# Six output tiles accumulated during the first modulation, x normed in place, and a final turn by transposes

## The chip, the cores and the metric

The kernel runs on one core of one Trainium2 chip. The metric is device time in microseconds. PE is TensorE, DVE VectorE, ACT ScalarE, POOL GpSimd, and SP the engine whose queue issues all loads and stores.

## What is computed

One inference step of a backbone of two layers over 384 tokens: 128 context tokens and 256 latent ones, width 1024, all in fp32.

```
mod = silu(cond) @ w_mod + b_mod              # shift, scale, gate, twice; per layer
h   = rmsnorm(x) * (1 + scale1) + shift1
q, k, v, gates, conv inputs, merge gates = h @ w_in
mix = sum over 3 branches of sigmoid(merge gate) * branch(h)   # DeltaNet, short conv, attention
x   = x + gate1 * rmsnorm(mix @ w_out)
x   = x + gate2 * rmsnorm(relu(h2 @ w_up)**2 @ w_down)         # h2 like h, from x
```

Outputs are y for all tokens, and keys, values and DeltaNet states of the context tokens. Nothing of h can be made before the modulation of its channels, and every other product of a layer needs h.

## The kernel before

**Products.** Each large product is made of three fp32r products: a high and a low half of the weights (wh, wl) and of the activations (HH, HL, or ah, al) give high x high, high x low and low x high. The functions FM (channels on the partitions, 8 x 3 products of 384 columns for one output tile), TM (tokens on the partitions; keys and values have 272 columns) and TMW record them. `fetch` loads a chunk of weights into wr (4 buffers), ACT casts the high half and DVE subtracts the low one (3 buffers each). All products write to 8 PSUM banks: 4 called mm, 4 called ax.

**Opening of layer 0.** `setup` loads the condition, x (8 tiles xt of 128 channels by 384 tokens) and constants. `first_norm` squares the tiles on ACT, adds them up in turn on DVE and POOL, and takes means by PE; `bcast` spreads the inverse norm into a bank (rb). `modquarter(q)` makes shift and scale for two channel tiles: 16 matmuls of 256 columns, with the condition as stationary operand in one of four column groups of the array, whose weights come as six loads (ws) through 8 buffers; `finish` copies the sums to rows and turns them with small products against sel2. `make_h(k)` makes h of tile k. The first FM tiles (keys, queries and values of head 0) have their products recorded tile by tile behind the four quarters. `turn_x` transposes x into tokens (om) behind the second quarter. Constants that are needed later are loaded once the last modulation matmul has been made (`hold`).

**Order.** All work is recorded first; a list scheduler (`schedule`) then gives every engine a fixed order, by the priority of a class (crit, st, gemm, ev, w, bg and others), by modelled durations (`cost`) and by a modelled transfer: rate, latency and issue time of the queue. On the chip an engine executes in that order and waits for what is late. While nothing else can run ahead of the first large product, and at three other places, PE makes filler products on ones.

**Body.** Behind keys and values come the heads: DeltaNet on DVE and POOL in small steps, and between them PE work from a list (`fills`): query groups, gates of the attention branch (`evac_mg` keeps their tanh in xt), branch projections. Then `split` makes high (ACT) and low halves (POOL) of the DeltaNet output ot, `merge` combines, w_out and the MLP follow. Modulation pieces for later stages are summed in between, partly on DVE (macc).

**End.** `post` takes the last product of a token block (OT), `newton` the inverse norm on single columns (ns), and `finish_y` turns x + gate * rmsnorm(...) back to channels: 8 products of x with the identity, 8 of the update with a diagonal matrix dg, accumulated in two banks, copied to yst and stored.

## Time and profile before

| what | us |
|---|---|
| median of 3 runs | 1985.2 (1985.07 to 1986.72) |
| the profiled execution | 1986.29 |
| its span, first to last instruction | 1984.6 |
| PE busy | 1957.0 |
| DVE busy | 1405.9 |

The span is what the views cover; start and times in them count from its first instruction. A busy PE includes the filler, and a product's time in a row is longer than its distance to the next one, since products are pipelined. All instructions have one line (L1778, where the recorded calls are made), so they are told apart by their tiles: `mm<-HH,wl` is a product into an mm bank from activations HH and low weights.

### The profile page before, as it was taken

The numbers are of one execution on the slowest core, as the hardware profiler recorded it, in microseconds if no ns is written. First come the engines' busy times: TensorE is split into PE (matmuls) and PEld (weight loads), VectorE is DVE, ScalarE is ACT, GpSimd is POOL, SyncE is SP. The second block draws the span as 40 slices with busy tenths as digits, with TensorE's granted clock in tenths as the row PEclk, the third lists the DMA queues.
The fourth block names the chain that finished last, engine by engine and source line by source line (L and its number), as shares of the span: only waits on it lengthen the run. The fifth ranks groups of instructions, "written<-read, shape, count | busy, mean of one in ns | idle before, by whom it ended". The sixth has DMA issues, their size and how long they took to land.

```text
span 1984.6 us, 35881 instructions
## 1 busy us (share of the span) xinstructions
PE 1957.0 (99%) x12980; PEld 1806.7 (91%) x12980; DVE 1405.9 (71%) x4317; ACT 949.3 (48%) x2188; POOL 431.6 (22%) x666
## 2 busy tenths in 40 slices
PE   9999999999999999999999999999999999999999
PEld 6998999999998799779779989999999998898987
DVE  3798887988868589769557988779888545432433
ACT  4676644555542354334246665445555424443432
POOL 1222222123234313003012022222232322110210
PEclk9999999999999999999999999999999999999999
DMA  8522333333336837756654223333333334554352
GB/s 270 192 81 84 106 110 130 119 122 117 107 124 208 289 128 231 217 189 204 158 177 147 85 94 115 111 119 122 121 115 107 120 123 144 195 124 128 127 128 64
DMA packets 132385, 280.48 MB, mean 141 GB/s; under 512 B 12240, under 2 KB 80496, under 8 KB 132208
## 3 DMA queue, kind: packets, MB, share of 16 engines
q1 hardware_dynamic: 132208, 278.19, 43.0%
q8 instruction: 102, 1.67, 0.3%
q14 instruction: 75, 0.61, 0.1%
HBM read 270.73 MB, written 7.42 MB: 140 GB/s over the span
## 4 chain that ended last, share of the span: by engine, by line
PE 83%; DVE 7%; DMA 4%; ACT 3%; issue 2%; POOL 0%; SPq 0%; DVEq 0%; ACTq 0%
PE mm L1778 70%; PE ax L1778 14%; DMA wr<-in_wmod 3%; DVE wl L1778 2%; DVE macc L1778 2%; ACT E L1778 1%; DVE q L1778 1%; ACT wh L1778 0%; DVE MB L1778 0%; ACT ht L1778 0%; ACT junk L1778 0%; DVE Xc L1778 0%; DVE Pr L1778 0%; DVE XT L1778 0%; DMA ws<-in_wmod 0%
## 5 line engine op out<-in xcount | busy, mean ns | idle before, releaser
L1778 DVE TENSOR_TENSOR wl<-wr,wh 128x1024 fp32r<-128x1024 f32 (+2 forms) x380 | 478.7, 1261 | 307.0 <-ACT wh L1778 305.8
L1778 ACT CAST wh<-wr 128x1024 fp32r<-128x1024 f32 (+2 forms) x380 | 396.0, 1043 | 559.3 <-PE mm L1778 454.1
L1778 PE MATMUL mm<-HH,wl 128*128 128x384 f32 x1664 | 568.9, 342 | 1.7 <-DVE wl L1778 1.7
L1778 PE MATMUL mm<-HL,wh 128*128 128x384 f32 x1664 | 567.7, 341 | 0.0
L1778 PE MATMUL mm<-HH,wh 128*128 128x384 f32 x1664 | 564.9, 340 | 0.6 <-ACT HH L1778 0.6
L1778 PEld LDWEIGHTS mm<-HH,wl 128*128 128x128 f32 x1664 | 312.9, 188 | 9.6 <-issue 4.5
L1778 PEld LDWEIGHTS mm<-HL,wh 128*128 128x128 f32 x1664 | 312.8, 188 | 6.5 <-issue 3.9
L1778 PEld LDWEIGHTS mm<-HH,wh 128*128 128x128 f32 x1664 | 312.4, 188 | 5.7 <-issue 1.2
L1778 DVE SCALAR_TENSOR_TENSOR macc<-wr,csil,macc 128x1024 f32<-128x1024 f32 x98 | 144.9, 1512 | 26.7 <-DMA wr<-in_wmod 26.7
L1778 PE MATMUL mm<-wh,HH 128*128 128x256 f32 (+1 forms) x480 | 139.9, 292 | 2.1 <-DVE eq L1778 1.4
L1778 PE MATMUL mm<-wl,HH 128*128 128x256 f32 (+1 forms) x480 | 139.4, 291 | 1.3 <-DVE wl L1778 1.3
L1778 PE MATMUL mm<-wh,HL 128*128 128x256 f32 (+1 forms) x480 | 140.1, 292 | 0.0
L1778 DVE TENSOR_TENSOR Pr<-MB,Xc 128x6 f32<-128x6 f32 (+30 forms) x496 | 138.7, 280 | 0.3
L1778 DVE TENSOR_REDUCE Xc<-Pr 128x6 f32<-128x12 f32 (+30 forms) x496 | 127.4, 257 | 7.7
L1778 DVE STREAM_SHUFFLE MB<-Mc 128x6 f32<-128x6 f32 (+30 forms) x496 | 131.7, 272 | 0.0
L1778 PE MATMUL mm<-al,wh 128*128 128x384 f32 x384 | 129.9, 339 | 1.6 <-POOL al L1778 1.5
L1778 PE MATMUL mm<-ah,wl 128*128 128x384 f32 x384 | 130.0, 339 | 0.2 <-DVE wl L1778 0.2
L1778 PE MATMUL mm<-ah,wh 128*128 128x384 f32 x384 | 130.0, 339 | 0.0
L1778 PE MATMUL mm<-wh,u 128*128 128x512 f32 x384 | 124.0, 399 | 0.0
L1778 PE MATMUL mm<-wh,ah 128*128 128x512 f32 x288 | 112.9, 392 | 0.0
L1778 PE MATMUL mm<-wh,al 128*128 128x512 f32 x288 | 112.7, 391 | 0.0
L1778 PE MATMUL mm<-wl,ah 128*128 128x512 f32 x288 | 112.5, 390 | 0.0
(270 smaller groups left out, 3314.8 us busy)
## 6 DMA issues: line engine op xcount, KB each, us to landing
wr<-in_wf SPq DMA_DIRECT2D x336, 512.0 KB, 3.3
wr<-in_wmod SPq DMA_DIRECT2D x80, 512.0 KB, 4.2
wr<-in_wq SPq DMA_DIRECT2D x16, 512.0 KB, 3.4
wr<-in_wdg SPq DMA_DIRECT2D x16, 512.0 KB, 3.3
ws<-in_wmod SPq DMA_DIRECT2D x16, 384.0 KB, 7.0
E<-scr SPq DMA_DIRECT2D x16, 384.0 KB, 3.6
Qe<-scr SPq DMA_DIRECT2D x16, 256.0 KB, 3.8
wr<-in_wkv SPq DMA_DIRECT2D x8, 408.0 KB, 5.7
```

Source lines behind the costliest of these rows:

```text
L1778: o.call(*o.a, **o.k)
```

## The change

Six output tiles (keys, queries, values of head 0, and three gates of the attention branch) are accumulated in six banks over the four quarters: `firstproducts(q)` makes the products of the two channel tiles of quarter q for all six, from two chunks of 768 columns (kind a), and evacuates them after the last quarter. The gates go out of the list of fills in layer 0. A modulation quarter loads all of one piece, then all of the other, into one bank. x is turned and then normed in place before the quarters, and h of context tokens is made on DVE, of latent tokens on ACT. Square sums are added in pairs and summed by PE. x comes in four loads, three constants come later.

Low halves of the DeltaNet output are made on DVE (`split_out`). In the second layer the three parts of the key weights are one group (`whole`). `finish_y` adds the residual on DVE and transposes the sum. The planner's model of transfers and of the small products is changed, and a class sp added. The diff, cut:

```diff
-                return n * 4 / 2.4 + 3 if op.k["tile_position"] == (0, 0) else 27.0
+                return n * 0.965 + 3 if op.k["tile_position"] == (0, 0) else 27.0
...
-    return max(56.0, n * outs[0].shape[0] * 4 / 360.0)
+    return max(56.0, n * outs[0].shape[0] * 4 / 385.0)
...
-    hw = 650.0
+    hw = 1000.0
...
-            dma = max(dma, hw + 650) + o.cost
+            dma = max(dma, hw + 1300) + o.cost
...
+        **{(e, "sp"): 1000 for e in ("ACT", "DVE")},
...
+        elif kind == "a":
+
+            src = aps["wf"][0, W_DK:W_DV + 1:8] if key[2] == 0 else aps["wf"][0, W_MG + 16:W_MG + 19]
+            src, n = src[:, :, 256 * key[1]:256 * key[1] + 256].rearrange("o p c -> p o c"), 768
...
-        dma = SP.dma_start(raw.rearrange("p (f c) -> p f c", f=4) if kind in "od" else raw[:, :n], src)
+        dma = SP.dma_start(raw[:, :n].rearrange("p (f c) -> p f c", c=256) if kind in "oda" else raw[:, :n], src)
...
-    def tok_means(ps, col, *srcs):
-
-        n = 3 * len(srcs)
-        for j, src in enumerate(srcs):
-            for t in range(3):
-                PE.matmul(ps[:, col:col + 3], lhsT=src[:, t * P:(t + 1) * P], rhs=sel[:, t, :],
-                          start=3 * j + t == 0, stop=3 * j + t == n - 1)
...
-    def split(k, src):
+    def split(k, src, eng=POOL):
         ACT.copy(a_hi[k], src)
-        POOL.tensor_tensor(out=a_lo[k], in0=src, in1=a_hi[k].bitcast(F32), op=SUB)
+        eng.tensor_tensor(out=a_lo[k], in0=src, in1=a_hi[k].bitcast(F32), op=SUB)
...
             def run(ch):
-                hi, lo = ch[0]
-                if j == 0:
+                if js[0] == 0:
...
                 for t in range(3):
                     ps = st["ps"][t]
                     rec.cls = "gemm"
-                    for i, k in enumerate(parts[j]):
...
+                    for (hi, lo), j in zip(ch, js):
+                        for i, k in enumerate(parts[j]):
+                            ah = h_hi[k][:, t * P:(t + 1) * P]
+                            al = h_lo[k][:, t * P:(t + 1) * P]
+                            wh, wl = hi[:, i * n:(i + 1) * n], lo[:, i * n:(i + 1) * n]
...
-        for j in range(len(parts)):
-            G([(kind, l, g, j)], part(j))
+        n_ = len(parts)
+        for js in [tuple(range(n_))] if whole else [(j,) for j in range(n_)]:
+            G([(kind, l, g, j) for j in js], part(js))
...
-        for k in range(8):
-            SP.dma_start(xt[k], aps["x"][:, k, :])
-        for t_, n_ in ((sel, "sel"), (ident, "ident"), (sel2, "sel2"), (bmod, "bmod"), (gn, "gn")):
+        for k in range(0, 8, 2):
+            SP.dma_start(XT[:, k:k + 2, :], aps["x"][:, k:k + 2, :])
+        for t_, n_ in ((sel, "sel"), (ident, "ident")):
...
+    def early_consts():
+        rec.cls = "w"
+        for t_, n_ in ((sel2, "sel2"), (bmod, "bmod"), (gn, "gn")):
+            SP.dma_start(t_, aps[n_])
+        rec.cls = "bg"
...
-        def run_part(j):
+        def run_part(p, j):
             def run(ch):
                 rec.cls = "st"
-                if j == 0:
-                    st["ps"] = axtile(), axtile()
+                if p + j == 0:
+                    st["ps"] = axtile()
                 for i, k in enumerate(KPARTS[j]):
                     c = k % 4
-                    for p in range(2):
-                        S["mm"] = PE.matmul(st["ps"][p][32 * c:32 * c + 32, :256], lhsT=csil[:, k, :],
-                                            rhs=ch[p][:, i], start=k < 4, stop=k > 3, tile_position=(0, 32 * c))
-                if j == 2:
+                    S["mm"] = PE.matmul(st["ps"][32 * c:32 * c + 32, 256 * p:256 * p + 256], lhsT=csil[:, k, :],
+                                        rhs=ch[0][:, i], start=k < 4, stop=k > 3, tile_position=(0, 32 * c))
+                if p and j == 2:
                     finish()
                 rec.cls = "bg"
             return run
...
         def finish():
+            row = dnp.tile([P, 4, P], F32, tag="vd" if q % 2 else "Qe", name="modrow")
+            ACT.copy(row.rearrange("p a b -> p (a b)"), st["ps"])
             ps = axtile()
-            for p in range(2):
-                row = trt("modrow")
-                ACT.copy(row[:, :256], st["ps"][p][:, :256])
-                for b in range(2):
-                    PE.matmul(ps[:, 4 * p + 2 * b:4 * p + 2 * b + 2], lhsT=row[:, b * P:(b + 1) * P], rhs=sel2,
-                              start=True, stop=True)
+            for i in range(4):
+                PE.matmul(ps[:, 2 * i:2 * i + 2], lhsT=row[:, i], rhs=sel2, start=True, stop=True)
             v = ps[:, :8].rearrange("p (i b c) -> p i c b", i=2, b=2)
             s = slice(2 * q, 2 * q + 2)
             for c in range(2):
                 DVE.tensor_tensor(out=mod[:, 0, 0:2, c, s], in0=v[:, :, c], in1=bmod[:, 0, 0:2, s], op=ADD)
+            for c in range(2):
                 DVE.scalar_tensor_tensor(out=gpre[:, 0, 0, c, s], in0=mod[:, 0, 1, c, s], scalar=1.0,
                                          in1=gn[:, 0, 0, s], op0=ADD, op1=MUL)
-        return [([("s", p, q, j) for p in range(2)], run_part(j)) for j in range(3)]
+        return [([("s", p, q, j)], run_part(p, j)) for p in range(2) for j in range(3)]
...
+    def firstproducts(q, evacs):
+
+        def part(i):
+            def run(ch):
+                if q == 0:
+                    S["first", i] = [axtile() if i and o else mmtile() if i or o else bank() for o in range(3)]
+                hi, lo = ch[0]
+                for o in range(3):
+                    ps, first = S["first", i][o], len(rec.ops)
+                    rec.cls = "gemm"
+                    for b in range(2):
+                        k, c = 2 * q + b, 256 * o + 128 * b
+                        wh, wl = hi[:, c:c + P], lo[:, c:c + P]
+                        PE.matmul(ps[:, :T], lhsT=wh, rhs=h_hi[k], start=k == 0, stop=False)
+                        PE.matmul(ps[:, :T], lhsT=wh, rhs=h_lo[k], start=False, stop=False)
+                        PE.matmul(ps[:, :T], lhsT=wl, rhs=h_hi[k], start=False, stop=k == 7)
+                    cold(first)
+                    if q == 3:
+                        rec.cls = "ev"
+                        evacs[3 * i + o](ps)
+                    rec.cls = "bg"
+            return run
+        return [([("a", q, i)], part(i)) for i in range(2)]
...
-    def make_h(rb, k):
+    def make_h(k):
 
         t = trt("ht")
-        rec.cls = "crit" if k < 2 else "bg"
-        DVE.tensor_tensor(out=t, in0=rb[:, :T], in1=xt[k], op=MUL)
+        rec.cls = "crit"
         for c, (a, b) in enumerate(STREAMS):
             g, sh = gpre[:, 0, 0, c, k:k + 1], mod[:, 0, 0, c, k:k + 1]
-            if k > 0:
-                ACT.activation(out=t[:, a:b], in_=t[:, a:b], func=AF.Identity, scale=g, bias=sh)
+            if c:
+                ACT.activation(out=t[:, a:b], in_=xt[k][:, a:b], func=AF.Identity, scale=g, bias=sh)
             else:
-                DVE.tensor_scalar(out=t[:, a:b], in0=t[:, a:b], scalar1=g, scalar2=sh, op0=MUL, op1=ADD)
-        ACT.copy(h_hi[k], t)
+                DVE.tensor_scalar(out=t[:, a:b], in0=xt[k][:, a:b], scalar1=g, scalar2=sh, op0=MUL, op1=ADD)
+        if k % 2:
+            ACT.copy(h_hi[k], t)
+        else:
+            DVE.tensor_copy(h_hi[k], t)
         DVE.tensor_tensor(out=h_lo[k], in0=t, in1=h_hi[k].bitcast(F32), op=SUB)
         rec.cls = "bg"
...
     def first_norm():
 
-        acc = kqp.tile([P, T], F32, tag="QT", name="acco")
+        rec.cls = "sx"
+        ps = axtile()
         for k in range(8):
-            sq = acc if k == 0 else trt("sq")
+            sq = trt("sq")
             ACT.activation(out=sq, in_=xt[k], func=AF.Square)
-            add_to(acc, k, POOL if k % 2 else DVE, sq)
-        ps = axtile()
-        tok_means(ps, 0, acc)
+            if k % 2:
+                DVE.tensor_tensor(out=sq, in0=sq, in1=last, op=ADD)
+                for t in range(3):
+                    PE.matmul(ps[:, 0:3], lhsT=sq[:, t * P:(t + 1) * P], rhs=sel[:, t, :],
+                              start=k + t == 1, stop=k == 7 and t == 2)
+            last = sq
+        rec.cls = "crit"
         sx = S["sx"] = small("n_sx")
         DVE.tensor_scalar(out=sx, in0=ps[:, 0:3], scalar1=EPS, scalar2=None, op0=ADD)
         S["rb"] = bcast(rsqrt3(sx))
+        rec.cls = "bg"
+
+    def norm_x():
+
+        rec.cls = "crit"
+        for k in range(8):
+            DVE.tensor_tensor(out=xt[k], in0=S["rb"][:, :T], in1=xt[k], op=MUL)
+        rec.cls = "bg"
...
     def turn_x():
 
         rec.cls = "sx"
         for t in range(3):
             for g in range(2):
-                ps = axtile()
+                ps = mmtile()
...
     def finish_y(t, n):
 
-        banks = [axtile() for _ in range(2)]
-        cols = [(slice(f * P, (f + 1) * P), banks[f // 4][:, f % 4 * P:f % 4 * P + P]) for f in range(8)]
-        for f, c in cols:
-            PE.matmul(c, lhsT=xm[:, t, f], rhs=ident, start=f.start % 512 == 0, stop=False)
-        dg = diag(t, *newton(n, 0))
-        for f, c in cols:
-            PE.matmul(c, lhsT=om[:, t, f], rhs=dg, start=False, stop=f.stop % 512 == 0)
-            if t == 2 and f.start == 512:
-                cold(len(rec.ops) - 1)
-        for g, ps in enumerate(banks):
+        y, z = newton(n, 0)
+        r = n[:, 5:6]
+        DVE.tensor_tensor(out=r, in0=z, in1=y, op=MUL)
+        rec.cls = "crit" + S["u"]
+        for g in range(2):
+            ps = axtile()
+            h = slice(512 * g, 512 * g + 512)
+            DVE.scalar_tensor_tensor(out=xm[:, t, h], in0=om[:, t, h], scalar=r, in1=xm[:, t, h], op0=MUL, op1=ADD)
+            for j in range(4):
+                f = 4 * g + j
+                PE.transpose(ps[:, j * P:(j + 1) * P], xm[:, t, f * P:(f + 1) * P], ident)
+                if t == 2 and f == 4:
+                    cold(len(rec.ops) - 1)
...
-        st = {}
+        st = {"kq": kqp, "at": atp, "dn": dnp}
 
         def pre0():
             first_norm()
+            turn_x()
+            norm_x()
...
-            st["kq"], st["at"], st["dn"] = kqp, atp, dnp
...
+        def split_out(f):
+            rec.cls = "sp"
+            split(f, ot[f], DVE)
+            rec.cls = "bg"
...
+            evacs = [evac_qkv(0, w) for w in (1, 0, 2)] + [evac_mg(f, True) for f in range(3)]
             for q in range(4):
-                items.extend(modquarter(q))
+                mq = modquarter(q)
+                items.extend(mq[:3])
+                if q == 0:
+                    X(early_consts)
+                items.extend(mq[3:])
                 for k in (2 * q, 2 * q + 1):
-                    X(lambda k=k: make_h(S["rb"], k))
-                if q == 1:
-                    X(turn_x)
-                if q:
-                    PRE([("w", l, (W_DK, W_DQ, W_DV)[q - 1])])
-            X(hold)
-            X(late_consts)
+                    X(lambda k=k: make_h(k))
+                if q == 3:
+                    X(hold)
+                    X(late_consts)
+                items.extend(firstproducts(q, evacs))
...
-        if l == 0:
-            qkv(0)
-        TM("k", l, 0, 272, evac_k)
+        TM("k", l, 0, 272, evac_k, l > 0)
...
-        fills += [(1, lambda f=f: FM(l, W_MG + 16 + f, hacts, evac_mg(f, True))) for f in range(8)]
+        fills += [(1, lambda f=f: FM(l, W_MG + 16 + f, hacts, evac_mg(f, True))) for f in range(3 * (l == 0), 8)]
...
-            X(lambda f=f: split(f, ot[f]))
+            X(lambda f=f: split_out(f))
```

## Rows read from the trace of the kernel before

**Rows 1.** the page: busy time of the engines, and the chain that ended last

```profile
PE 1957.0 (99%) x12980; PEld 1806.7 (91%) x12980; DVE 1405.9 (71%) x4317; ACT 949.3 (48%) x2188; POOL 431.6 (22%) x666
...
PE 83%; DVE 7%; DMA 4%; ACT 3%; issue 2%; POOL 0%; SPq 0%; DVEq 0%; ACTq 0%
```

**Rows 2.** stages, us busy: PE, PEld, DVE, ACT, POOL; then PEclk, DMA share, GB/s

```profile
20.00:30.00 10.00, 9.31 (x72) 5.97 (x71) 6.25 (x14) 4.44 (x8) 0.00 (x0) 1.00 1.09 370
30.00:40.00 10.00, 9.39 (x82) 6.71 (x82) 2.94 (x9) 7.61 (x15) 0.00 (x0) 1.00 0.45 152
...
100.00:120.00 20.00, 19.69 (x151) 18.42 (x151) 18.27 (x88) 15.01 (x50) 6.37 (x13) 1.00 0.26 89
```

**Rows 3.** PE in order of time, opening: start, time, what, [wait]

```profile
21.13 1.20 PE L1778 MATMUL ax<-sel,modrow 128*128 128x2 f32 x8
...
26.03 0.44 PE L1778 MATMUL mm<-HH,wh 128*128 128x384 f32 x1
...
28.41 0.63 PE L1778 MATMUL ax<-ws,csil 128*32 128x256 f32 x6
28.97 0.45 PE L1778 MATMUL mm<-HL,wh 128*128 128x384 f32 x1
29.34 0.63 PE L1778 MATMUL ax<-ws,csil 128*32 128x256 f32 x4
...
33.09 1.47 PE L1778 MATMUL ax<-ident,XT 128*128 128x128 f32 x12
...
37.85 2.18 PE L1778 MATMUL ax<-ws,csil 128*32 128x256 f32 x32
...
41.40 1.05 PE L1778 MATMUL ax<-sel,modrow 128*128 128x2 f32 x8
...
47.02 0.63 PE L1778 MATMUL ax<-ws,csil 128*32 128x256 f32 x4
...
55.57 0.29 PE L1778 MATMUL mm<-wh,HH 128*128 128x272 f32 x1
```

**Rows 4.** the load queue in order of time, opening

```profile
1.52 3.95 SPq L1778 DMA_DIRECT2D XT<-in_x  x8
...
8.37 4.60 SPq L1778 DMA_DIRECT2D ws<-in_wmod  x8
```

**Rows 5.** waits of the load queue to 70 us: total, times, longest

```profile
SPq L1778 <- PE ax L1778: 15.2, 9, 7.5
```

**Rows 6.** PE in order of time, start of the last MLP

```profile
1706.66 1.05 PE L1778 MATMUL ax<-ident,XT 128*128 128x128 f32 x8
...
1712.09 0.34 PE L1778 MATMUL mm<-HH,wh 128*128 128x384 f32 x1
...
1717.46 0.33 PE L1778 MATMUL mm<-HL,wh 128*128 128x384 f32 x1
```

**Rows 7.** the chain that ended last, its end: start, time, what

```profile
1968.29 5.40 PE ax L1778 x48
```

**Rows 8.** DVE in order of time, at the end

```profile
1974.90 0.69 DVE L1778 TENSOR_TENSOR OT<-mm,OT 128x512 f32<-128x512 f32 x1 [0.48 <-PE mm L1778]
...
1978.03 0.35 DVE L1778 TENSOR_SCALAR dg<-ident,ns 128x128 f32<-128x128 f32 x1
```

**Rows 9.** groups by line: busy us, mean ns, idle before

```profile
L1778 POOL TENSOR_TENSOR al<-OT,ah 128x384 fp32r<-128x384 f32 x16 | 23.1, 1472 | 7.7 <-ACT ah L1778 7.7
...
L1778 DVE SCALAR_TENSOR_TENSOR XT<-OT,ns,XT 128x512 f32<-128x512 f32 x18 | 12.9, 748 | 0.3
...
L1778 DVE TENSOR_TENSOR al<-ax,ah 128x384 fp32r<-128x384 f32 x16 | 8.8, 552 | 5.4 <-ACT ah L1778 5.4
```

**Rows 10.** waits of PE over the span: total, times, longest

```profile
PE ax L1778 <- DVE macc L1778: 7.9, 4, 4.2
...
PE mm L1778 <- POOL al L1778: 1.5, 2, 1.1
```

**Rows 11.** a stage behind the longest wait of PE

```profile
855.00:860.00 5.00, 5.00 (x24) 2.62 (x23) 0.57 (x1) 0.37 (x1) 0.00 (x0) 0.54 0.63 213
```

More of the change, by code (lines that the diff above doesn't have):

```diff
@@ L655, in FM, with TM, part @@
         G([("w", l, row)], run)
-    def TM(kind, l, g, n, evac):
+    def TM(kind, l, g, n, evac, whole=False):
         st = {}
         parts = KPARTS if kind == "k" else HALVES
-        def part(j):
+        def part(js):
             def run(ch):
-                hi, lo = ch[0]
-                if j == 0:
+                if js[0] == 0:
                     st["ps"] = [bank(), mmtile(), mmtile()]
@@ L671, in run @@
                     rec.cls = "gemm"
[L672 to L678 removed]
+                    for (hi, lo), j in zip(ch, js):
[3 more added lines that the diff above has]
+                            wh, wl = hi[:, i * n:(i + 1) * n], lo[:, i * n:(i + 1) * n]
+                            PE.matmul(ps[:, :n], lhsT=ah, rhs=wh, start=k == 0, stop=False)
+                            PE.matmul(ps[:, :n], lhsT=ah, rhs=wl, start=False, stop=False)
+                            PE.matmul(ps[:, :n], lhsT=al, rhs=wh, start=False, stop=k == 7)
                     cold(first)
@@ L751, in late_consts @@
     def late_consts():
-        for t_, n_ in ((utri, "utri"), (ltri, "ltri"), (delta, "delta"), (rc, "rc"), (rs, "rs"), (cdn, "cdn"),
+        for t_, n_ in ((cdn, "cdn"), (utri, "utri"), (ltri, "ltri"), (delta, "delta"), (rc, "rc"), (rs, "rs"),
                        (csc, "csc"), (gdn, "gdn"), (gqc, "gqc")):
```

6 lines of the change are left out of this document (removed).

## The prediction

> **What bounds the kernel now.** I read the page first. TensorE (PE) is busy for 99% of the span, and 83% of the chain that ended last is PE work [rows 1]. So a microsecond of PE work, or a wait of PE, that goes away anywhere in the body should come off the end, unless another engine has just as much to do there. The kernel has one order written by a planner, and each engine keeps to it; a wait of PE cannot be filled with other work once the order stands.
>
> The table by stage comes next, because busy is not useful: before the first weights arrive PE runs filler products on ones. The opening ends when the first three output tiles (keys, queries and values of head 0) are complete, at 55.57, where the first product with 272 columns starts [rows 3]. Those tiles are 72 products of 384 columns. One takes 0.173 us: 31 steps lie between the two rows of the long run, (1717.46 - 1712.09) / 31 [rows 6]. So 55.6 us have bought 72 x 0.173 = 12.5 us of large products. What holds it is the modulation: its weights are two pieces of 1024 x 1024 in fp32, 8.4 MB, in four quarters; h of a quarter exists only after its matmuls, and the last of these starts at 47.02 [rows 3]. The stream could be faster: 370 GB/s from 20 to 30 us, but 152 from 30 to 40 [rows 2], where the load queue sat 7.5 us in one wait for PE to free a modulation buffer [rows 5].
>
> The end is the second place. The chain there shows 48 PE pieces, 5.40 us in one block, ahead of the last products of token block 2 [rows 7]: the final turn of blocks 0 and 1, and the identity half of block 2.
>
> **The change part by part.**
>
> **Opening: start.** The queue now issues cond, four x loads instead of eight, and two constants ahead of the modulation. Eight x issues took 3.95, 0.49 each, and the first modulation load went out at 8.37 [rows 4]. Now it goes at about 1.52 + 6 x 0.49 = 4.4, 4.0 earlier. The norm loses its serial walk through GpSimd, x is normed and turned before h is needed, and all of that is covered by the wait for the first quarter. I move the first large product from 26.03 [rows 3] to 22.0. Bounds: no gain, because x is as late as before (26.0); or 20.5, if the shorter norm counts too.
>
> **Opening: six tiles.** Instead of 72 products 144 are made before the keys, as 36 per quarter: 36 x 0.173 = 6.2 us. The opening is now to be measured against 55.57 + 12.5 = 68.0, the time at which the old kernel would have made the same 144. Beside them PE has, in each later quarter, the modulation matmuls and the small products with sel2. The latter are 8 records, 1.05 [rows 3]. The former were 2.18 when one quarter ran in one piece. They come with six loads, though, and when they run apart each group takes 0.56 (28.41 to 28.97) and the large product between two groups holds PE for 0.37 (28.97 to 29.34) in place of 0.173, 0.2 more [rows 3]. Six such groups are 6 x 0.76 = 4.6. Between 2.2 and 4.6 I take 3.6, since in three of the four quarters of before they ran apart. A later quarter is then 6.2 + 3.6 + 1.0 = 10.8. From 22.0: 22.0 + 6.2 + 3 x 10.8 = 60.6, against 68.0: a gain of 7.4.
>
> Two bounds. By the stream: 8.4 MB, six of the eight new chunks of 0.39 MB, 1.6 MB of x and 0.3 of constants are 12.7 MB; at 370 GB/s [rows 2] 34 us, from about 2 us on. If PE keeps up, the last modulation matmul ends near 38 to 40, and the old distance from its end to the last of 36 products, 55.57 - 47.65 = 7.9 [rows 3], gives 48: a gain of 20. From the other side: first product at 26.0, groups apart, 26.0 + 6.2 + 3 x 11.8 = 67.6: a gain of 0.4. I stay by the PE sum, since 10.8 per quarter is more than the stream's (2.1 + 0.8) MB / 370 GB/s = 7.8.
>
> Between two modulation groups a large product costs 0.2 more than in a row of its kind [rows 3, 6]. The Trainium skill, page TensorEngine Tiling (Array Packing), section Key Properties, speaks against such interleaving: a change of tiling mode drains the TensorE. By that rule the price stands at each change and the sum with it; were changes free and the groups as cheap as in one piece (2.2), the opening would end at 56.4 and the kernel take 1966. The trace agrees with the rule, with its 0.2.
>
> **Opening: what is given back.** Three of the six tiles are gates of the attention branch, which used to fill PE among the first heads. From 100 to 120 DVE was busy for 18.27 of 20 us [rows 2]; there PE loses cover and DVE becomes the limit. Three tiles are 12.5 us of PE work; over the layer PE has far more to spare it, so I charge 1.5 (bounds: 0, and 6, half of that work). Six evacuations also fall together at the end of the opening instead of one by one; they hold four of the banks that the keys need. The keys wait at most for one conversion chain, and I leave that inside the 1.5. Net opening: -5.9.
>
> **Final turn.** Each output block was 8 products with the identity and 8 with a diagonal, two records each; now DVE adds the residual in two instructions of 0.75 [rows 9] and PE makes 8 transposes, 0.12 each (12 in 1.47) [rows 3]. The 5.40 block in front of the last products goes, and block 0's transposes, 1.0, may still come ahead of them. The tail behind the last product stays as long as it was: it began at 1974.90 with the add on DVE and had its diagonal at 1978.03 [rows 8]; in place of 0.35 for the diagonal and 16 records it has 0.2 for one small product, 0.75 twice, and eight transposes that overlap the second. DVE's additions for blocks 0 and 1, 3.0 us, now run beside block 2's chain; I charge 0.4 for one that is in its way. Net -4.0, bounds -2.0 and -5.4.
>
> The identity products of blocks 0 and 1 had been pulled far ahead, into the start of the last MLP: three groups of 8 records like the one at 1706.66 [rows 6], each 8 x 5.40 / 48 = 0.9 [rows 7]. PE has no wait of its own there, so I take them as on the path: -2.7. Bound: 0, if the modulation weights of that stage pace it.
>
> **Low parts.** The low halves of the delta output move from GpSimd, 1.47 each, to DVE; the like DVE instruction takes 0.55 [rows 9]. In the trace PE waits on GpSimd for them 1.5 in all [rows 10], in the first layer alone. DVE gets 8 x 0.55 = 4.4 more at a point where it feeds modulation sums as well, and loses GpSimd beside it. I take -0.8; bounds -1.5 and +2.9 (the 4.4 in full, less the 1.5).
>
> **Keys.** In the second layer the three weight parts are used as one group, token block by token block. The planner could already order it so; the price is that all three split buffers are held until the third block. Cost nothing, bounds -1 and +1: it is hidden by the modulation matmuls of that stage.
>
> **Plan.** The planner's transfer latency goes from 650 to 1300 ns and its rate from 360 to 385. Where PE was sent too early to products of the modulation sums it waits 4.2 in one place [rows 10] and runs at a granted clock of 0.54 afterwards [rows 11], that is largely at the 1.2 GHz level. A later due time should shorten such waits; I take -1.4, bounds -7 (both gone) and +5 (one more like it).
>
> Sum: -5.9 - 4.0 - 2.7 - 0.8 + 0 - 1.4 = -14.8. The profiled execution took 1986.3 (span 1984.6), so 1971.5; the median of the runs is 1.1 below that execution, so 1970.
>
> **The rivals.**
>
> Stream-bound opening: PE keeps up, all six tiles are done near 48. For it: nothing but PE frees the buffers, and the x turn no longer stands in its way. Against: 10.8 of PE per quarter against 7.8. Opening -20 + 1.5, the rest -8.9: 1986.3 - 27.4 - 1.1 = 1958.
>
> Opening given back: the quarters run apart, the first product is no earlier, and DVE takes the rest among the first heads. For it: 18.27 of 20 on DVE [rows 2]. Opening +1.1 (-0.4 + 1.5), the rest -8.9: 1986.3 - 7.8 - 1.1 = 1977. If also the groups at 1706.66 and the plan yield nothing, the end alone is left, -3.7: 1981.5.
>
> Slower: filler stops at the first large product, so from then on a wait of PE is bare. If h of each later quarter comes late, PE stands for 4.2 as it does at the sums and loses 3 more at the lower clock. That is 7.2 x 3 = 21.6, and the opening ends at 82 instead of 60.6: -5.9 + 21.6 - 8.9 = +6.8, 1992. It decides when the opening ends after 76. Against: there are 6.2 us of products of the quarter before to cover a chain that took 4.9 from 21.13 to 26.03 [rows 3].
>
> **How the numbers follow.** Forecast, between 1963 and 1977: 0.55. Stream-bound, below 1963: 0.13. Given back, 1977 to 1989: 0.25, of which 0.17 lies below 1981. Slower: 0.07. This kernel's measurement can tell 0.2%, 4.0 us, so faster means below 1981.2: 0.55 + 0.13 + 0.17 = 0.85; same 0.08; slower 0.07. The range leaves out a tenth on each side: 1960 to 1982.
>
> **What would show it.** The last modulation matmul before 45 instead of 47.6, and the first product with 272 columns near 61; no wait of the load queue near 7 us. No block of ax pieces ahead of the last products; these end 4 to 5 us nearer to the body. No PE wait on low parts. Wrong would be: PE waits of several us between quarters, a clock below 1 after 26 us, the gain of the opening gone by 150 us, or a new wait of PE for modulation sums.

## The result, and the profile after

| kernel | median of runs, us | ratio to before | 95% interval |
|---|---|---|---|
| before | 1985.96 (1985.07 to 1991.18) | | |
| changed | 1962.22 (1960.42 to 1967.68) | 0.9891 | 0.987 to 0.9912 |

The change makes the kernel 1.1% faster: 23.7 us, inside the range of the prediction and 8 us below its likeliest value. The profiled execution of the changed kernel is the longest of its four runs, 1967.68 with a span of 1965.2. Its mean granted clock is 0.996, like that of the run of 1963.94; the two runs near 1960.5 have 0.998. The traces below put that difference in the opening; of those two runs there is no trace.

The page of the changed kernel, busy time and the chain that ended last:

```profile
PE 1947.7 (99%) x12918; PEld 1800.4 (92%) x12918; DVE 1418.8 (72%) x4352; ACT 945.0 (48%) x2176; POOL 402.2 (20%) x646
...
PE 88%; DVE 5%; DMA 3%; ACT 2%; issue 1%; POOL 1%; DVEq 0%; ACTq 0%; POOLq 0%; SPq 0%
```

PE's busy time fell by 9.3 from [rows 1], the rest of the span (span less PE) from 27.6 to 17.5. So about half of the gain in span, 19.4, is busy time that went (filler and slow clock counted in), and half is waiting that went.

Its stages, columns as in [rows 2]:

```profile
20.00:30.00 10.00, 10.00 (x95) 7.30 (x91) 6.86 (x18) 5.70 (x10) 0.00 (x0) 0.97 0.93 295
30.00:40.00 10.00, 10.00 (x70) 6.75 (x70) 5.39 (x13) 3.76 (x6) 0.00 (x0) 1.00 0.93 298
100.00:120.00 20.00, 20.00 (x164) 19.33 (x163) 15.92 (x56) 16.91 (x63) 7.25 (x13) 1.00 0.42 134
800.00:805.00 5.00, 2.37 (x10) 1.39 (x8) 3.09 (x4) 1.24 (x2) 0.00 (x0) 1.00 0.90 275
805.00:810.00 5.00, 3.94 (x17) 1.88 (x20) 3.33 (x3) 1.05 (x1) 0.00 (x0) 0.56 0.93 274
810.00:815.00 5.00, 5.00 (x26) 3.41 (x20) 2.85 (x5) 0.71 (x2) 0.00 (x0) 0.76 0.68 172
855.00:860.00 5.00, 5.00 (x23) 4.04 (x22) 1.23 (x1) 1.66 (x2) 0.00 (x0) 1.00 0.58 203
```

From 30 to 40 us the transfers run at 298 instead of 152 GB/s. From 100 to 120, where I feared for DVE, its busy time fell from 18.27 to 15.92, and from 855 to 860 the clock is full where [rows 11] had 0.54. But the low clock has not gone: it stands some 50 us earlier, 0.56 and 0.76 from 805 to 815. There are two waits on modulation sums here in both kernels. Before, PE was idle for 1.4 us at 807 and 4.2 at 849; now it is idle for 3.7 at 802 and 0.9 at 848, so the long one has changed places and the low clock with it.

PE in order of time in the opening, the rows that answer to [rows 3]:

```profile
10.40 1.40 PE L1830 MATMUL ax<-sel,sq 128*128 128x3 f32 x12
...
30.49 0.80 PE L1830 MATMUL mm<-HH,wh 128*128 128x384 f32 x3
...
51.85 0.62 PE L1830 MATMUL ax<-ws,csil 128*32 128x256 f32 x4
...
67.81 0.29 PE L1830 MATMUL mm<-wh,HH 128*128 128x272 f32 x1
```

The first large product comes at 30.49, not at the 22.0 of the forecast and even later than before. From there the six tiles take 37.3 (forecast 38.6). The opening ends at 67.81; 68.0 was the time at which the old kernel would have made the same products. In this execution it gained next to nothing, 0.3.

Waits of PE over the span, then of the load queue to 70 us, to be held against [rows 10] and [rows 5]:

```profile
PE ax L1830 <- DVE macc L1830: 5.1, 4, 3.7
PE ax L1830 <- ACT PT L1830: 1.2, 1, 1.2
```

```profile
SPq L1830 <- DVE wl L1830: 13.1, 6, 6.4
SPq L1830 <- PE ax L1830: 8.6, 8, 4.1
```

The wait on modulation sums is shorter (5.1 for 7.9), and its longest, 3.7, is the one at 802. That on POOL for low halves is gone. The queue's longest wait for a modulation buffer is 4.1 instead of 7.5; its longest of all is now 6.4, for a buffer of weights that DVE has yet to split.

The end on DVE, for [rows 8]:

```profile
1957.09 0.16 DVE L1830 TENSOR_TENSOR ns<-ns 128x1 f32<-128x1 f32 x1
1957.29 1.41 DVE L1830 SCALAR_TENSOR_TENSOR XT<-OT,ns,XT 128x512 f32<-128x512 f32 x2
...
1959.51 0.69 DVE L1830 COPY yst<-ax 128x512 f32<-128x512 f32 x1 [0.21 <-PE ax L1830]
```

The diagonal is gone and two additions stand in its place, 1.41 for both; the last copy starts 21.0 earlier than before (1980.52 there).

**Where the time comes off.** The same instruction stands in all the traces, so its start can be compared. The table gives, in us, start in that kernel less start in the kernel before; the head of a column is the time of the instruction in the trace of before. The kernels other than "changed" are the experiments below.

| kernel | 492.0, last heads, layer 0 | 729.9, first MLP | 910.1 | 1386.6, heads, layer 1 | 1637.2 | 1725.0, last MLP | span |
|---|---|---|---|---|---|---|---|
| changed | -2.5 | -6.9 | -7.4 | -12.0 | -12.2 | -17.1 | -19.4 |
| old_opening | -2.7 | -9.2 | -10.4 | -14.2 | -14.5 | -19.4 | -22.3 |
| old_low_parts | -7.1 | -12.8 | -13.7 | -18.3 | -18.5 | -23.3 | -26.1 |
| old_keys | -3.7 | -6.8 | -7.4 | -10.3 | -10.5 | -15.2 | -18.2 |
| old_turn | -4.6 | -10.3 | -11.5 | -16.1 | -16.3 | -17.3 | -17.3 |
| plan_alone | -1.6 | -6.4 | -8.4 | -10.8 | -11.1 | -12.1 | -12.2 |
| plan_transfers | -3.9 | -9.2 | -14.1 | -14.9 | -15.2 | -15.5 | -15.6 |
| old_plan | -6.5 | -6.5 | -6.7 | -9.4 | -9.5 | -13.5 | -16.5 |
| three_tiles | -0.4 | -6.4 | -9.1 | -14.1 | -14.4 | -19.2 | -22.3 |
| means3 | -7.1 | -13.3 | -16.8 | -21.1 | -21.3 | -25.9 | -28.9 |

Each row is one execution. Two that should be equal up to a point differ there by 2 to 5 us, so a step within one row says more than a difference between rows. From 730 to 910, where PE waits for modulation sums, the changed kernel gains only 0.5.

The changed kernel was not run again beside the experiments. The kernel before was, 11 times with each set of them, and its median there is 1988.13 to 1988.83 instead of 1985.96. A difference between an experiment's median and 1962.22 can be off by as much as these medians differ.

### The profile page after: what moved, and what is told of

Same layout as the page of the kernel before. It is cut to its first block, busy times and chain, and to the rows that moved or that the text cites. A ratio compares the mean times of both kernels' runs of the same rounds, so it can differ in the third digit from the quotient of the medians.

```text
span 1965.2 us, 35744 instructions
## 1 busy us (share of the span) xinstructions
PE 1947.7 (99%) x12918; PEld 1800.4 (92%) x12918; DVE 1418.8 (72%) x4352; ACT 945.0 (48%) x2176; POOL 402.2 (20%) x646
## 4 chain that ended last, share of the span: by engine, by line
PE 88%; DVE 5%; DMA 3%; ACT 2%; issue 1%; POOL 1%; DVEq 0%; ACTq 0%; POOLq 0%; SPq 0%
PE mm L1830 74%; PE ax L1830 14%; DMA wr<-in_wmod 2%; DVE wl L1830 1%; DMA wr<-in_wf 1%; DVE macc L1830 1%; ACT wh L1830 0%; POOL xe L1830 0%; DVE MB L1830 0%; DVE XT L1830 0%; DMA E<-scr 0%; ACT mm L1830 0%; ACT ht L1830 0%; DVE c L1830 0%; DVE Pr L1830 0%
## 5 line engine op out<-in xcount | busy, mean ns | idle before, releaser
L1830 PE MATMUL mm<-HL,wh 128*128 128x384 f32 x1648 | 562.0, 341 | 0.0
L1830 PE MATMUL mm<-HH,wl 128*128 128x384 f32 x1648 | 559.8, 340 | 0.4 <-DVE wl L1830 0.4
L1830 PE MATMUL mm<-HH,wh 128*128 128x384 f32 x1648 | 559.1, 340 | 0.0
```

Of the source, the lines that this page charges most:

```text
L1830: o.call(*o.a, **o.k)
```

## The experiments

**One old part at a time.** Four kernels take one part of the change back and keep the rest.

old_opening: `setup`, `first_norm`, `modquarter`, `make_h`, `turn_x` and the order of the items of layer 0 are those of before.

> The changed kernel with the opening of the kernel before (x loads in eight pieces, norm through GpSimd and VectorE, three output tiles before the keys); final turn, low parts, keys and the planner's numbers stay changed. As forecast, the opening is worth 5.9 us net: this kernel takes 1962.2 + 5.9 = 1968. By the shift between the two profiled executions it is worth 2.5: 1965. Rival, the opening is worth nothing on this chip or less, since its clock was at half speed from 14 to 20 us: 1962 or below. In the profile the first large product should start near 26 us, against 30.5 with the new opening, and the last heads of layer 0 should come 2.5 us later than in the changed kernel by the second theory, 6 by the first.

Measured: 1964.41 (1963.75 to 1965.36), 0.9883 (0.9861 to 0.9905). That is 2.2 above the changed kernel by the medians; above its two runs with the same mean clock, 0.998, it is about 4. Against the kernel before, each in its own set, the two are alike (0.9883 and 0.9891). The first large product is at 25.61, as expected; the shift at the last heads of layer 0 is -2.7, the same as in the changed kernel's profile. So in that execution the shift is not the new opening's: the old one has it too, with the new plan.

old_low_parts:

```diff
-            X(lambda f=f: split_out(f))
+            X(lambda f=f: split(f, ot[f]))
```

> The changed kernel with the low halves of the delta output of both layers on GpSimd again. As forecast, the move to VectorE is worth 0.8 us: 1963. By the shift between the two profiled executions, which grows from 2.5 us at the last heads of layer 0 to 5.8 us behind the output products of the delta branch, it is worth 3.3: 1965.5. Rival: the shift there belongs to another part (the plan, or gates that were made early), and this kernel takes 1962 with the shift unchanged. In the profile TensorE should wait on GpSimd for low halves again, 1.5 us in all by the trace of before.

Measured: 1962.44 (1960.4 to 1967.3), 0.9875 (0.9852 to 0.9899). Moving the low halves is worth nothing (0.2): no wait of PE on POOL's low halves shows in this trace either, and the shift grows by 5.7 from 492 to 730 with the old low parts, 4.4 with the new. The theory of 3.3 fell. The forecast's 0.8 lies within the scatter, but the wait that it was to come from is not there, so the rival fits best.

This execution also shows the new opening undisturbed. Granted clock (third from the right) in the changed kernel's profile, 12 to 22 us:

```profile
12.00:14.00 2.00, 2.00 (x20) 1.28 (x15) 0.00 (x0) 0.00 (x0) 0.00 (x0) 0.92 1.14 318
14.00:16.00 2.00, 2.00 (x10) 1.18 (x10) 0.00 (x0) 0.00 (x0) 0.00 (x0) 0.50 1.11 319
16.00:18.00 2.00, 2.00 (x12) 1.08 (x12) 0.65 (x4) 0.58 (x1) 0.86 (x1) 0.50 0.89 302
18.00:20.00 2.00, 2.00 (x12) 1.34 (x12) 0.00 (x0) 0.59 (x1) 0.00 (x0) 0.50 1.10 367
20.00:22.00 2.00, 2.00 (x18) 1.07 (x12) 0.00 (x0) 0.58 (x1) 0.00 (x0) 0.87 0.99 343
```

and the same stretch, then PE in order of time, with old low parts:

```profile
14.00:16.00 2.00, 2.00 (x20) 1.18 (x21) 0.56 (x4) 1.03 (x2) 0.86 (x1) 1.00 0.97 300
16.00:18.00 2.00, 2.00 (x19) 1.13 (x14) 0.00 (x0) 0.72 (x2) 0.00 (x0) 1.00 1.04 351
```

```profile
9.18 1.40 PE L1830 MATMUL ax<-sel,sq 128*128 128x3 f32 x12
...
26.19 0.80 PE L1830 MATMUL mm<-HH,wh 128*128 128x384 f32 x3
...
63.51 0.29 PE L1830 MATMUL mm<-wh,HH 128*128 128x272 f32 x1
```

The instructions and their order are the same. Ahead of the fall PE made the means, 12 products of three columns with two records each, in turn with modulation products; in one execution the clock is at its lower level (1.2 GHz) from 14 to 20 us and for part of the slices on both sides, in the other it is not. The first large product is 4.3 later, 1.2 by the start of the small products and 3.1 at the lower clock, and the end is 4.3 later too (67.81 against 63.51): nothing catches up. The kernel before had a fall too (0.64 from 16 to 18, 0.51 from 18 to 20), but its opening ended within 0.5 of that of old_opening, whose clock stayed full (55.57 and 55.14).

old_keys:

```diff
-        TM("k", l, 0, 272, evac_k, l > 0)
+        TM("k", l, 0, 272, evac_k)
```

> The changed kernel with the keys and values of the second layer in three groups of weight parts again. As forecast the whole group is worth 0 us, with bounds of 1 on each side: 1962. By the shift between the two profiled executions, which grows from 8.2 us at the layer's boundary to 12.0 us among its first heads, the keys can be worth up to 3.8: 1966. Rival: that shift comes with the planner's later due times; then 1962 here, and it goes when the planner's old numbers are put back.

Measured: 1961.18 (1958.21 to 1968.15), 0.9865 (0.9841 to 0.9889): not to be told from the changed kernel. From 910 to 1387 the shift grows by 2.9 with the keys in three groups, by 4.6 in the changed kernel: 1.7 for the whole group by these two traces, and the rest of that step is another part's.

old_turn: `finish_y` of before.

> The changed kernel with the final turn of the kernel before (identity products and diagonal products on TensorE in place of additions on VectorE and transposes). As forecast, the new turn is worth 4.0 us at the end and 2.7 at the start of the last MLP: 1962.2 + 6.7 = 1968.9. By the shift between the two profiled executions 3.9 and 4.9: 1971. Rival: the identity products at the start of the last MLP only filled waits for weights, and the end alone counts: 1966.

Measured: 1965.53 (1960.93 to 1969.96), 0.989 (0.9867 to 0.9913), 3.3 above the changed kernel. The trace gives more. From 1637 to 1725 its shift grows by 1.0, that of the changed kernel by 4.9: 3.9 for the identity products at the start of the last MLP. From 1725 to the end it grows by nothing, against 2.3. The last copy starts 3.9 nearer to the body in the changed kernel (21.0 - 17.1), but the end of the span comes 5.7 behind that copy instead of 4.1 (1980.52 to 1984.6; 1959.51 to 1965.2). About 1.0 of these 1.6 comes with the new turn: the eight other kernels that have it end 4.95 to 5.36 behind the copy, the five with the old turn 4.03 to 4.09. The two copies of the last block now start 0.49 apart instead of 0.89; whether that is the reason was not tried.

Four parts taken back cost 2.2, 0.2, -1.0 and 3.3, 4.7 in all, of 25.9 in their set. The rest seemed left to the planner's numbers.

**The plan.** plan_alone is the kernel before with four numbers changed:

```diff
-                return n * 4 / 2.4 + 3 if op.k["tile_position"] == (0, 0) else 27.0
+                return n * 0.965 + 3 if op.k["tile_position"] == (0, 0) else 27.0
...
-    return max(56.0, n * outs[0].shape[0] * 4 / 360.0)
+    return max(56.0, n * outs[0].shape[0] * 4 / 385.0)
...
-    hw = 650.0
+    hw = 1000.0
...
-            dma = max(dma, hw + 650) + o.cost
+            dma = max(dma, hw + 1300) + o.cost
```

> The kernel before with nothing but the planner's four new numbers (cost of a small tiled product, transfer rate, first issue and latency). As forecast they are worth 1.4 us: 1985 where the kernel before takes 1986. By what the four kernels with one old part each leave over (1988.1 - 1962.2 = 25.9 in that set, less 2.2 for the opening, 0.2 for the low parts, -1.0 for the keys and 3.3 for the turn), the numbers are worth up to 21: 1966. Rival: parts that stand in for each other when one is undone; then the numbers alone bring some 5 to 10, 1976 to 1981. In the profile the waits of TensorE on modulation sums (7.9 us) and on low halves of weights (3.2) should be shorter, and the granted clock from 850 to 860 us at full.

Measured: 1973.81 (1970.08 to 1974.83) against 1988.45, 0.9924 (0.9902 to 0.9945). Four numbers in a table bring 14.6 us by themselves. The waits on modulation sums are still 6.0 here, and the low clock is not gone either: 0.76 from 805 to 810.

old_plan is the changed kernel with the four old numbers.

> The changed kernel with the planner's four numbers of before. As forecast it loses 1.4: 1963.6. By what the other parts leave over it loses up to 21: 1983. Rival, in between: the other parts shorten the same waits, and it loses 5 to 10: 1967 to 1972. In the profile the wait on modulation sums near 850 us and half the clock behind it should be back in the second and third cases, and not in the first.

Measured: 1971.82 (1968.35 to 1976.13), 0.9917 (0.9894 to 0.9939): it loses 9.6, the case in between. The rest of the change, without the planner's numbers, is thus 16.6 below the kernel before (1988.45), somewhat more than the numbers alone; the two halves overlap, and the four parts taken back one at a time (4.7) understate the rest.

The clock is 0.59 from 845 to 850 us and 0.73 from 850 to 855, and the wait on modulation sums is 5.9. So the long wait is back at the second of the two places. But the changed kernel has 5.1 and its own low clock behind the first, so that is not where the 9.6 lie. The rows of the table show more: from 730 to 910 old_plan gains 0.2 and the changed kernel 0.5, but from 492 to 730 it gains nothing where the changed kernel gains 4.4, and from 910 to 1387 2.7 against 4.6. A part of it is this wait of PE in the trace of old_plan, on weights whose high half is not cast yet, which the changed kernel's list does not have:

```profile
PE mm L1830 <- ACT wh L1830: 1.8, 1, 1.8
```

plan_cost has the first of the four numbers alone, plan_transfers the other three, both on the kernel before.

> The kernel before with one of the planner's four new numbers: the cost of a small tiled product (the modulation's in the opening and at the sums), 250 instead of 430 ns for 256 columns. The four together bring 14.6 us in plan_alone (1988.4 to 1973.8). If this one does it, the planner places the modulation's products and the work around them better: 1974 to 1976. If the transfer numbers do it, 1986 to 1990 here. Rival: each brings a part, 1979 to 1983.

> The kernel before with the planner's three new numbers for transfers alone (rate, first issue, latency of 1300 instead of 650 ns). If later due times for transfers do it, TensorE's waits on weights (3.2 us on low halves, 3.2 on transfers of the modulation in the trace of before) and on modulation sums (7.9) get shorter, and the kernel takes 1974 to 1976. If the products' cost does it, 1986 to 1990. Rival: each a part, 1979 to 1983.

Measured: plan_cost 1981.56 (1977.36 to 1982.91), 0.9961 (0.9948 to 0.9974); plan_transfers 1970.85 (1970.33 to 1972.63), 0.9912 (0.9898 to 0.9926). The transfers' numbers do it, -18.0, somewhat more than expected; the products' cost has some 7 alone and nothing on top (plan_alone, with both, has 14.6).

Waits of PE in plan_transfers, against [rows 10]:

```profile
PE ax L1778 <- DVE macc L1778: 3.1, 3, 1.8
PE ax L1778 <- DMA wr<-in_wmod: 2.3, 3, 1.2
PE mm L1778 <- DVE wl L1778: 1.5, 2, 1.3
```

All the waits that the view lists sum to 10.8, against 22.7 before. Span less busy PE is 15.6 instead of 27.6, so 12.0 of the 15.6 by which this span is shorter is waiting that went. Most of the other 3.6 can be the clock: the kernel before has 0.64 and 0.51 from 16 to 20 us and 0.78 and 0.54 from 850 to 860, plan_transfers full clock there and 0.73 and 0.92 from 800 to 810. As an estimate, the missing shares times the lengths make 5.1 and 1.8 us, 3.3 apart. One place, 850 to 855 us, before and then in plan_transfers:

```profile
850.00:855.00 5.00, 1.70 (x4) 0.80 (x5) 3.04 (x3) 1.04 (x1) 0.00 (x0) 0.78 0.57 219
```

```profile
850.00:855.00 5.00, 5.00 (x23) 4.04 (x22) 2.77 (x3) 1.64 (x2) 0.00 (x0) 1.00 0.65 210
```

Before, PE stood for 3.3 of 5 us, and the five behind them are [rows 11]; now it has products to make. At the first of the two places, from 795 to 805, PE still stands for 1.8.

**The opening.** norm2_first gives six of the eight multiplications of the norm a lower priority than the work on h; the planner then leaves four in front:

```diff
-        rec.cls = "crit"
         for k in range(8):
+            rec.cls = "crit" if k < 2 else "bg"
             DVE.tensor_tensor(out=xt[k], in0=S["rb"][:, :T], in1=xt[k], op=MUL)
```

> The changed kernel with only the first two multiplications of the norm ahead of the modulation's addition and of h on VectorE; the other six come behind them. Theory 1, the first large product is late because eight of them (22.92 to 26.73) stand in front of h: it comes some 2 us earlier, and the kernel takes 1960 to 1961. Theory 2, it is late because TensorE's granted clock is 0.50 from 14 to 20 us in executions like the profiled one (30.49, against 26.19 in the profiled execution of the kernel with old low parts, which has the same opening at full clock): then the order on VectorE brings under 1, and the scatter of 7 us between executions stays. Rival: what is won at the opening's start is lost by 70 us, since the modulation's weights or TensorE's own work end the opening: 1962.

Measured: 1959.24 (1958.77 to 1961.07), 0.9857 (0.9834 to 0.988). DVE in order of time, in the changed kernel and then here:

```profile
22.92 3.81 DVE L1830 TENSOR_TENSOR XT<-ax,XT 128x384 f32<-128x384 f32 x8 [5.09 <-PE mm L1830]
26.65 0.22 DVE L1830 TENSOR_TENSOR mod<-ax,bmod 128x4 f32<-128x4 f32 x2
```

```profile
18.94 1.95 DVE L1830 TENSOR_TENSOR XT<-ax,XT 128x384 f32<-128x384 f32 x4 [3.02 <-PE mm L1830]
20.81 0.22 DVE L1830 TENSOR_TENSOR mod<-ax,bmod 128x4 f32<-128x4 f32 x2
```

The eight stand in front of the addition of the modulation's constant, and they wait for PE to have turned x. With four in front the addition comes behind 1.95 instead of 3.81, and the first large product is at 24.32: 1.9 before the 26.19 at the same full clock. Only 0.3 of that is left where the six tiles end (63.21 against 63.51). The best runs are 1.7 better than those of the changed kernel; theory 1 holds at the start, and its rival for most of the rest. The scatter of 7 that theory 2 expects is not there: the six runs lie within 2.3, with mean clocks of 0.997 to 0.999.

means3 makes the square sums on DVE, one product for each token block:

```diff
-            if k % 2:
+            if k:
                 DVE.tensor_tensor(out=sq, in0=sq, in1=last, op=ADD)
-                for t in range(3):
-                    PE.matmul(ps[:, 0:3], lhsT=sq[:, t * P:(t + 1) * P], rhs=sel[:, t, :],
-                              start=k + t == 1, stop=k == 7 and t == 2)
             last = sq
+        for t in range(3):
+            PE.matmul(ps[:, 0:3], lhsT=last[:, t * P:(t + 1) * P], rhs=sel[:, t, :], start=t == 0, stop=t == 2)
```

> The changed kernel with the squares of x summed on VectorE (3 products of three columns instead of 12) and the norm in its place, all eight multiplications ahead of h. If the small products ahead of the norm let the clock fall, it stays at 1.00 from 12 to 22 us here, the first large product comes near 26 in each execution, and the kernel takes 1960 with little scatter. If the order of VectorE is all that counts in means3_norm2, this one is as the changed kernel: 1962 with a scatter of 7. If the sums are bad for the norm, it is later than 1962.

> The changed kernel with the order of norm2_first, and with the squares of x summed on VectorE, so that the means take 3 products of three columns instead of 12. Theory 1 (order of VectorE alone): as norm2_first, 1960 to 1961. Theory 2 (the clock): TensorE makes filler products where it made small ones, the granted clock from 12 to 22 us stays at 1.00, the first large product comes at 24 to 26 us in each execution, and the kernel takes 1957 to 1959 with less scatter. Rival: the serial sums on VectorE delay the norm by as much as the clock gives: 1962, with the clock at 1.00 or not.

Measured: means3 1957.99 (1954.95 to 1960.94), 0.9849 (0.9832 to 0.9865); means3_norm2 1958.0 (1956.89 to 1959.18), 0.9848 (0.9822 to 0.9873). Both are faster than the kernel before by 1.5% and than the changed one by 4.2 of the medians. In both profiles the granted clock is 1.00 from 12 to 26 us, and none of their nine runs has a mean clock below 0.998. That the three products in place of twelve do this is likely, not shown: norm2_first keeps the twelve, and none of its six runs was at 0.996 either, while of 25 runs of the changed kernel, old_low_parts, old_keys, old_turn and three_tiles nine were. The first large product is at 25.54 and 23.91, the six tiles end at 64.42 and 62.82. The serial sums thus cost little, and the order of the norm adds nothing that the times can tell, though its six tiles end 1.6 earlier.

three_tiles makes three tiles in the opening:

```diff
-        return [([("a", q, i)], part(i)) for i in range(2)]
+        return [([("a", q, 0)], part(0))]
...
-        fills += [(1, lambda f=f: FM(l, W_MG + 16 + f, hacts, evac_mg(f, True))) for f in range(3 * (l == 0), 8)]
+        fills += [(1, lambda f=f: FM(l, W_MG + 16 + f, hacts, evac_mg(f, True))) for f in range(8)]
```

> The changed kernel with three output tiles in the opening instead of six; the three gates are made among the first heads again, the rest of the opening is the new one. As forecast, six tiles give TensorE work while the modulation arrives: a later quarter with three takes at least the stream's time, some 7 to 8 us, so the first product with 272 columns starts at 26 + 3 + 3 x 7.7 = 52 and the 72 products made later cost 12.5: the whole is 1 to 2 us worse than with six, 1962 to 1964 at the clock of the kernel with old low parts. Theory 2, the early modulation alone makes the gain of 4 against the old opening, and six tiles give nothing: 1960. Rival: without the products of three more tiles TensorE waits in each quarter, as in the kernel before: 1964 to 1966, like the old opening.

Measured: 1962.92 (1960.51 to 1966.5), 0.9872 (0.9856 to 0.9888): 0.7 from six tiles. Its profile has the fall of the clock too (0.50 from 14 to 18), and PE in order of time shows:

```profile
30.86 0.78 PE L1830 MATMUL mm<-HH,wh 128*128 128x384 f32 x3
...
55.36 0.28 PE L1830 MATMUL mm<-wh,HH 128*128 128x272 f32 x1
```

With the 12.5 of the 72 products that come later this is 67.9, against 67.81 with six tiles. Three tiles need 24.5 from the first large product on, the old opening 29.5 (25.61 to 55.14) for the same products. So the second three tiles only move their own work. Of the 5.0 between 24.5 and 29.5, by the distances from row to row, 2.5 is the turn of x (24 records), which the old opening makes behind its first large product and the new one ahead of it, 1.1 are modulation products (64 records behind the first large product instead of 84), and the rest is the large products and the waits among them. The first large product is 5 us later here than in the old opening, so part of this may be the later start; three tiles at full clock were not seen.

## Why the prediction was right, and which steps of it were not

The direction and the range held, the account by parts did not: of the sum of -14.8 the largest term, the opening, was too large, and the plan's -1.4 far too small. These two misses have opposite signs, so it is in part luck that the time lies inside the range.

**What bounds the kernel.** Right: PE's order sets the end. Waiting that went came off the span (12.0 of 15.6 in plan_transfers).

**Opening: start** (26.03 to 22.0). Failed. The loads do go out early (4.57, forecast 4.4). But "all of that is covered by the wait for the first quarter" is wrong: the eight multiplications stand between the quarter's sums and its h, worth 1.9 by norm2_first, and they wait for the turn of x. Nor does the early load arrive in full: it goes out 3.8 earlier, but at full clock the first quarter's sums are turned only 0.8 earlier (19.08 in the trace with old low parts, 19.85 in old_opening), and the first large product comes 7.1 behind them instead of 5.8. 26.19 at full clock is my bound of no gain. 30.49 is outside it, since I had no case for the lower clock behind the means, although the trace of before has one in its opening (0.64 and 0.51 from 16 to 20).

**Opening: six tiles.** The length was right: 37.3 for a forecast of 38.6. Its gain was put in the wrong place. At full clock the opening gains 4.1 (63.51 against 55.14 + 12.5), and the forecast's 7.4 less the 4.2 of the failed start would be 3.2. three_tiles ends level with six, at the lower clock in both: the gain is not the tiles'. It is more likely the turn of x, which now runs ahead of the first large product, and the earlier modulation.

**Given back** (+1.5). None shown: with old low parts the undisturbed opening is 4.4 ahead of old_opening at 492 (-7.1 and -2.7), 4.1 at its own end. Net -5.9 became -2.2 by the medians, nothing by the ratios and about -4 at equal clock.

**Final turn** (-4.0 and -2.7). The mechanism was right and the sum near it by the trace, -2.3 and -3.9: the end lost 1.6 behind the last copy, which I took to stay as it was, and the identity products were wholly on the path, with more than their own 2.7. The medians give 3.3; the scatter leaves open which is nearer.

**Low parts** (-0.8). Measured nothing. The 1.5 of waits on POOL went with the plan, before the move could remove them. **Keys** (0, bounds of 1). Right by the times; the trace allows up to -1.7.

**Plan** (-1.4, bounds -7 and +5). The step that failed by most: -14.6 alone, -9.6 taken back, both beyond the bound. I priced one wait at modulation sums and the clock behind it [rows 10, 11], as if the plan's new numbers could reach nothing else. In the changed kernel that wait did not even go: the two waits there went from 5.5 to 4.6, the long one stands at 802 instead of 849, with the clock at 0.56 behind it, and the stretch from 730 to 910 gained 0.5. The gain came elsewhere, from 492 to 730 and from 910 to 1387 (4.4 and 4.6, with the old numbers 0.0 and 2.7). A due time stands behind every load, and all the waits of PE, 22.7, were in the same view. The profile of before had the test of the numbers too. Its groups of transfers (KB each, then median us from issue to landing):

```profile
wr<-in_wf SPq DMA_DIRECT2D x336, 512.0 KB, 3.3
...
gdn<-in_gdn SPq DMA_DIRECT2D x1, 1.0 KB, 2.4
```

Both planners count 0.475 us for the issue. With it the old one gave 512 KB 0.475 + 0.65 + 524.3 / 360 = 2.6 us, the new one gives 0.475 + 1.30 + 524.3 / 385 = 3.1; the chip takes 3.3 at the median, and 2.4 even for this 1 KB. The old plan thus counted on weights some 0.7 us before they were there. That later due times are what shortened the waits fits the rows; which of the three numbers did it was not taken apart. The Trainium skill, page DMA: Bandwidth & Descriptors, section Specifications, gives about 0.6 us to the first byte on the hardware path; whoever takes that for the time to landing gets the old number, and by the trace it is not. Its section Anatomy of one DMA names a fixed cost of about 2.0 us with the completion, for the GpSimd path; the 2.4 of this SP load is near that.

**Rivals.** The time falls by its number among the "stream-bound" cases, below 1963, but not for that reason: the six tiles ended at 63.5 at best (62.8 in means3_norm2), not near 48. "Opening given back" describes the profiled execution's opening (-0.3), which the plan more than made good. No wait of PE between quarters is listed, so "slower" never came near.

**The signs.** Held: no block of ax pieces ahead of the last products, no PE wait on low parts, the last products nearer to the body. Not held: the last modulation matmul starts at 51.85, 47.6 at full clock, and not before 45; the first product with 272 columns comes at 67.81 or 63.51, not near 61; the load queue still waits 6.4 in one place. Of the signs of being wrong, the clock is below 1 after 26 us, as it was before, and the long wait for modulation sums stands at another place.

**What stays open.** -14.6 (plan), -2.2, -3.3, -0.2 and +1.0 make -19.3 of -23.7; with the 9.6 of old_plan it is -14.3. By the traces, at equal clock, the opening has 4.1 and the turn 6.2, which with the 9.6 makes 19.9. The rest lies within the scatter of the medians, or in parts that stand in for each other: without the plan the rest of the change is worth 16.6. Why the clock falls in some executions and not in others was not settled; in six profiles with the twelve products and the new plan it fell in the four where the first of these came at 9.89 us or later, and stayed full in the two with 9.18 and 9.49. A still longer latency in the plan was not tried.

## What to carry to other kernels

When a diff touches the numbers of a planner, hold them against measured landings and durations first, and put all the waits of the bounding engine at stake, not the nearest. Run the constants by themselves: four numbers were worth more here than a rebuilt opening. When a wait is gone from its old place, look for it at the like places before and behind: the one for modulation sums stood 50 us earlier. On an engine that carries a sum on to the bounding one, keep work that is not yet needed behind that step.

## What the runs showed of the hardware

The same instruction order had a granted clock of 0.50 from 14 to 20 us in one execution and of 1.00 in another, behind the same 12 products of three columns; PE was busy all the time by the page's count in both. With 3 such products in their place it stayed at 1.00 in both profiles, and with 12 also in that of norm2_first. Three loads of 1 KB in the kernel before took 2.4, 2.6 and 3.5 us from issue to landing, its 336 loads of 512 KB 3.3 at the median.
